# Seven-product blocks kept in three stick-breaking groups per layer, with their products in another order; attention outputs spilled unsplit; the first loads in halves

## The chip, the cores and the metric

One core of a Trainium2 chip (trn2) runs the whole program; there is one launch, and the time is device time in microseconds. The kernel before took 2468.08 us in the median of three runs (2466.44 to 2469.51). The engines are TensorE (PE, with its weight loads as PEld), VectorE (DVE), ScalarE (ACT), GpSimd (POOL) and SyncE (SP); DMAs are issued from the queues of SP, POOL and, a few, ACT.

## What is computed

Two layers on a residual stream of 256 tokens by 2048 channels, all in float32. Each layer is one normalised input, one wide input projection, two attention branches, gates, and an output projection (the reference, cut):

```python
h = rms_norm(x, norm_gain)
proj = jnp.einsum('bsd,de->bse', h, w_in)            # 10 segments of 2048 columns
(da_q, da_k, da_v, da_z, sb_q, sb_k, sb_v, sb_z, gate_a, gate_b) = split_columns(proj)
# differential attention, 8 heads: rms_norm and rope on q and k, two softmaxes per head
a = probs(qb1, k1t) - lam * probs(qb2, k2t)
ua = rms_norm(a @ v, subln_gain) * (1 - lambda_init) * jax.nn.silu(da_z)
# stick-breaking attention, 16 heads
log_fail = jnp.where(strict, jax.nn.log_sigmoid(-z), 0.0)
after = lax.cumsum(log_fail, axis=3, reverse=True) - log_fail
w = jnp.where(strict, jnp.exp(jax.nn.log_sigmoid(z) + after), 0.0)
ub = (w @ v) * jax.nn.silu(sb_z)
y = jax.nn.sigmoid(gate_a) * (ua @ w_branch_a) + jax.nn.sigmoid(gate_b) * (ub @ w_branch_b)
return x + y @ w_out
```

## The kernel before, in words

**Weights and splits.** Every projection is cut into chunks of 512 output columns: 40 of the input projection per layer, and 4 each of the two branch projections and of the output projection. A chunk is 8 tiles (`kp`) of 128 x 1024 float32, 512 KB each, which hold two contraction slices of 128. A tile is loaded into `raw` (a ring of 11), and split (L63) into a rounded high part `wh` by ACT (L64, ring of 4) and a low part `wl` by DVE (L65, ring of 3). A product is then three matmuls (`mm3`, L69 to L71) of a 128 x 128 stationary activation and 512 weight columns: high by high, high by low, low by high.

**A plain chunk** is a `c_stream` (L102): 8 tiles, each used for the two token halves, so 8 x 2 x 2 x 3 = 96 matmuls. Its two sums stand in two PSUM banks, either the pair `mc` or (with `alt`) the pair `sU`, `sN`; at its end `fin` reads them out.

**A seven-product block** is an `s_stream` (L127): two chunks are multiplied together by a recursion in two halves of the contraction, two halves of the tokens and the two chunks, with seven half products in place of eight. One product is 4 tiles x 2 slices x 3 = 24 matmuls, so a block is 168 where two plain chunks are 192. The price is sums of weights: the block loads 12 tiles from SP, and makes sums of them in place with 12 more loads from POOL that add to what lies in the tile (`add_dma`, L145 to L147), and with 4 additions on DVE (`add_w`, L208, through L151). A summed tile is split anew, so that there are 28 splits. The products, named here by bank: the first (`sU`, tile set `xs`), the second (`sN`, set `zs`), the third (`sQ`, `xs` with its first addition), the fourth (more into `sU`, `xs` with its second addition, which is issued only as the third product has split the tile), the fifth (`sQ` once more, `zs` with its addition), and the last two. The sums of the left operand lie in `sm` (`left_sums`, L303).

**The order of the work.** `run` (L222) takes one step of this and one step of that stream, in proportion to their lengths; a step is one tile. A scheduler that simulates the engines then fixes the order of the instructions on each queue, and each engine's queue runs in that order. A layer is: differential attention in four groups of heads (plain chunks one after the other, attention between them; L683 to L695); stick-breaking attention in four groups (L707 to L733), each with a seven-product block of its V and Z chunks beside two plain chunks (the next group's Q and K, in group 3 the gates a0 and a1); then the branch projections (`a_stream` L749, `b_stream` L759), with seven-product blocks of the other six gate chunks beside them (L778 to L786); then four output chunks (L825 on). So there are 7 seven-product blocks in a layer, 14 in all, and 38 plain chunks per layer.

**What goes through DRAM.** The attention outputs are split on chip and spilled as two tensors by POOL (`spill`, L495), and read back by POOL in 8 pieces per branch and layer (`reload`, L699) when buffers come free. The gates' sigmoids (`sig_d`) and the gated first branch (`ya_d`) are spilled by POOL and read back by SP (L745) in the middle of the branch stream that needs them.

**The start.** `first_input` (L333) loads the transposed input, 256 KB per step, ahead of each of the first chunk's weight tiles, and ACT and DVE scale and split it (L339, L340).

## Time and profile before

| | |
|---|---|
| runs | 2468.08 us, median of 3 (2466.44 to 2469.51) |
| the profiled execution | 2464.42 us, its span 2462.7 us, granted clock 0.988 |
| PE, PEld busy | 2384.9 us (97%), 1965.0 us (80%) |
| DVE, ACT, POOL busy | 1743.6 us (71%), 1531.9 us (62%), 393.7 us (16%) |
| DMA | 571.21 MB, mean 232 GB/s |
| matmuls and transposes on PE | 10996 |

A matmul of 512 columns is shown as some 390 ns long, but the next one starts before it ends; so the busy share of PE says little, and the distance from one start to the next is what counts. "Idle before" with a releaser names what ended a wait. The stages that the text speaks of, in us from the span's start: differential attention of layer 1 at 1231 to 1590; stick-breaking groups 0 to 2 at 440 to 735 (layer 0) and 1663 to 1955 (layer 1); from stick-breaking group 3 to the last gate block at 735 to 1080 and 1955 to 2300.

### The profile page before, as it was taken

The numbers are of one execution on the slowest core, as the hardware profiler recorded it, in microseconds if no ns is written. First come the engines' busy times: TensorE is split into PE (matmuls) and PEld (weight loads), VectorE is DVE, ScalarE is ACT, GpSimd is POOL, SyncE is SP. The second block draws the span as 40 slices with busy tenths as digits, with TensorE's granted clock in tenths as the row PEclk, the third lists the DMA queues.
The fourth block names the chain that finished last, engine by engine and source line by source line (L and its number), as shares of the span: only waits on it lengthen the run. The fifth ranks groups of instructions, "written<-read, shape, count | busy, mean of one in ns | idle before, by whom it ended". The sixth has DMA issues, their size and how long they took to land.

```text
span 2462.7 us, 31649 instructions
## 1 busy us (share of the span) xinstructions
PE 2384.9 (97%) x10996; PEld 1965.0 (80%) x10996; DVE 1743.6 (71%) x1979; ACT 1531.9 (62%) x2214; POOL 393.7 (16%) x476
## 2 busy tenths in 40 slices
PE   8999999999999999899999999999999998997999
PEld 6888888788887777688888888887888877876887
DVE  5677767688787676575666776777887876766754
ACT  6666666677777555454565676667777775655543
POOL 1132230200101211200020321302101112112000
PEclk9999999999999999899999999999999999999999
DMA  9546646888988989987665465378889889899873
GB/s 338 174 141 225 197 137 232 210 239 229 247 239 246 296 266 274 293 315 250 212 207 180 151 221 187 119 249 208 247 238 229 247 248 295 281 289 264 320 233 102
DMA packets 163040, 571.21 MB, mean 232 GB/s; under 512 B 18624, under 2 KB 19136, under 8 KB 162880
## 3 DMA queue, kind: packets, MB, share of 16 engines
q1 hardware_dynamic: 120960, 423.55, 50.8%
q0 software_dynamic: 39328, 141.58, 24.9%
q10 hardware_dynamic: 2592, 4.07, 0.5%
q8 instruction: 86, 1.41, 0.2%
q14 instruction: 74, 0.61, 0.1%
HBM read 535.57 MB, written 33.55 MB: 231 GB/s over the span
## 4 chain that ended last, share of the span: by engine, by line
PE 67%; issue 17%; DMA 7%; POOL 4%; DVE 2%; ACT 2%; POOLq 0%; SPq 0%; ACTq 0%; DVEq 0%
PE mc L69 11%; PE mc L70 11%; PE mc L71 11%; DMA raw<-in_w_in 6%; PE sU L70 4%; PE sN L70 4%; PE sU L71 4%; PE sN L71 4%; PE sN L69 4%; PE sU L69 4%; POOL raw L147 2%; PE at L243 2%; PE sQ L70 1%; PE sQ L69 1%; PE sQ L71 1%
## 5 line engine op out<-in xcount | busy, mean ns | idle before, releaser
L65 DVE TENSOR_TENSOR wl<-raw,wh 128x1024 fp32r<-128x1024 f32 x1000 | 1209.8, 1222 | 495.3 <-PE mc L70 158.9
L64 ACT CAST wh<-raw 128x1024 fp32r<-128x1024 f32 x1000 | 1045.9, 1053 | 724.4 <-PE mc L71 280.9
L147 POOL DMA_DIRECT2D raw<-in_w_in x168 | 145.5, 868 | 743.0 <-DVE wl L65 466.3
L70 PE MATMUL mc<-wl,xTh 128*128 128x512 f32 x576 | 225.9, 392 | 0.4 <-DVE wl L65 0.2
L71 PE MATMUL mc<-wh,xTl 128*128 128x512 f32 x576 | 225.0, 391 | 0.0
L69 PE MATMUL mc<-wh,xTh 128*128 128x512 f32 x576 | 207.0, 394 | 5.5 <-ACT tok L465 3.4
L69 PE MATMUL mc<-wh,xrh 128*128 128x512 f32 x512 | 198.6, 392 | 8.6 <-ACT wh L64 8.5
L70 PE MATMUL mc<-wl,xrh 128*128 128x512 f32 x512 | 201.8, 394 | 1.8 <-DVE wl L65 1.8
L71 PE MATMUL mc<-wh,xrl 128*128 128x512 f32 x512 | 200.9, 392 | 0.0
L69 PEld LDWEIGHTS mc<-wh,xTh 128*128 128x128 f32 x576 | 107.8, 189 | 29.9 <-ACT wh L64 4.3
L70 PEld LDWEIGHTS mc<-wl,xTh 128*128 128x128 f32 x576 | 108.5, 188 | 25.6 <-DVE wl L65 3.5
L71 PEld LDWEIGHTS mc<-wh,xTl 128*128 128x128 f32 x576 | 108.5, 188 | 21.7
L69 PEld LDWEIGHTS mc<-wh,xrh 128*128 128x128 f32 x512 | 96.4, 189 | 29.3 <-ACT wh L64 9.5
L70 PEld LDWEIGHTS mc<-wl,xrh 128*128 128x128 f32 x512 | 96.6, 189 | 23.3 <-DVE wl L65 3.7
L71 PEld LDWEIGHTS mc<-wh,xrl 128*128 128x128 f32 x512 | 96.6, 189 | 19.2
L252 POOL TENSOR_SCALAR rv<-ssq 128x4 f32<-128x4 f32 (+1 forms) x48 | 40.2, 837 | 419.4 <-ACT junk L433 379.4
L70 PE MATMUL sU<-wl,xrh 128*128 128x512 f32 x256 | 100.6, 393 | 1.1 <-DVE wl L65 1.1
L71 PE MATMUL sN<-wh,xrl 128*128 128x512 f32 x256 | 100.5, 393 | 0.0
L70 PE MATMUL mc<-wl,ua 128*128 128x512 f32 x256 | 100.2, 391 | 0.2 <-DVE wl L65 0.2
L71 PE MATMUL sU<-wh,xrl 128*128 128x512 f32 x256 | 100.2, 391 | 0.0
L69 PE MATMUL sN<-wh,xrh 128*128 128x512 f32 x256 | 100.1, 391 | 0.0
L70 PE MATMUL sN<-wl,xrh 128*128 128x512 f32 x256 | 99.9, 390 | 0.0
(258 smaller groups left out, 5010.6 us busy)
## 6 DMA issues: line engine op xcount, KB each, us to landing
raw<-in_w_in SPq DMA_DIRECT2D x584, 512.0 KB, 4.4
raw<-in_w_in POOLq DMA_DIRECT2D x168, 512.0 KB, 9.7
raw<-in_w_a SPq DMA_DIRECT2D x64, 512.0 KB, 5.7
raw<-in_w_b SPq DMA_DIRECT2D x64, 512.0 KB, 5.8
raw<-in_w_o SPq DMA_DIRECT2D x64, 512.0 KB, 4.3
uah<-uh POOLq DMA_DIRECT2D x8, 512.0 KB, 4.9
ual<-ul POOLq DMA_DIRECT2D x8, 512.0 KB, 6.9
ubh<-uh POOLq DMA_DIRECT2D x8, 512.0 KB, 6.4
```

What stands on the lines that cost most here:

```text
L64: nc.scalar.copy(h, src)
L65: nc.vector.tensor_tensor(out=l, in0=src, in1=h.bitcast(F32), op=ALU.subtract)
L69: nc.tensor.matmul(ps, lhsT=lh, rhs=rh, start=start, stop=False, **kw)
L70: nc.tensor.matmul(ps, lhsT=lh, rhs=rl, start=False, stop=False, **kw)
L71: nc.tensor.matmul(ps, lhsT=ll, rhs=rh, start=False, stop=stop, **kw)
L147: nc.gpsimd.dma_start(out=dst, in_=src, accum_op=ALU.add)
L243: nc.tensor.transpose(out=tr[:, j * P:(j + 1) * P], in_=src[:, j * P:(j + 1) * P], identity=ident)
L252: nc.gpsimd.tensor_scalar(out=v[:, :w], in0=ss, scalar1=1.0 / n, scalar2=RMS_EPS, op0=ALU.mult, op1=ALU.add)
```

## The change

1. Seven-product blocks stay only in stick-breaking groups 0 to 2: 3 in a layer, 6 in all. Group 3's Z and V and all eight gate chunks become plain chunks, one stream at a time: Z, V, then gate a0, branch a0, gate a1, branch a1 and so on, then the same for b. A layer has 46 plain chunks.
2. In a seven-product block the product with `zs` that came fifth comes fourth, ahead of the one that adds to `sU`; it uses bank `sQ` again, right after the third product, whose result ACT copies out (L215).
3. Attention outputs are spilled as one float32 tensor, half the bytes. They are read back by SP into the `raw` ring and split then (one ACT and one DVE instruction per 512 KB). The last stick-breaking group's output isn't spilled; it stays on chip as the split pair, and branch b's streams start their contraction with it.
4. The first weight tile is loaded and split in two halves, the first input tile too, and DVE in place of ACT makes the high part of the latter.
5. The `raw` ring has 12 buffers, `ev` shares the `pp` ring of 5, and a doubled set of constants is gone.

```diff
-RAW = 11
+RAW = 12
...
+    def held(nm):
+        return wp.tile([P, CW], F32, name="pp", bufs=PPB)
...
+    def first_slice(src, between):
+        raw = raw_tile()
+        h = wp.tile([P, KK * CW], F32R, name="wh", bufs=4)
+        l = wp.tile([P, KK * CW], F32R, name="wl")
+        for i in range(KK):
+            c = slice(i * CW, (i + 1) * CW)
+            nc.sync.dma_start(out=raw[:, c], in_=src[:, c])
+            if i == 0:
+                between()
+            with tc.high_priority(offset=400):
+                split(h[:, c], l[:, c], raw[:, c])
+        return h, l
...
-    def c_stream(src, lhs, fin, alt=False, gap=0, before=None):
+    def c_stream(src, lhs, fin, alt=False, gap=0, before=None, first=False, depth=range(KP)):
...
-        for kp in range(KP):
-            if before is not None:
-                before(kp)
-            h, l = split_raw(load_raw(src[kp]))
+        for i, kp in enumerate(depth):
+            if first and i == 0:
+                h, l = first_slice(src[kp], lambda: before(0))
+            else:
+                if before is not None:
+                    before(i)
+                h, l = split_raw(load_raw(src[kp]))
...
-    def s_stream(sl, sr, xh, sm, fin):
+    def s_stream(sl, sr, xh, sm, fin, tb_dma=False):
...
         q_ps = ps_s.tile([P, CW], F32, name="sQ")
-        yield from prod(q_ps, s(0), lambda i: xs[i], lambda i: add_dma(xs[i], b22[i]))
+        yield from prod(q_ps, s(0), lambda i: xs[i], next_sums)
         p5 = held("p5")
         nc.scalar.copy(p5, q_ps)
         yield
+        if tb_dma:
+            v_ps = ps_s.tile([P, CW], F32, name="sQ")
+            yield from prod(v_ps, s(2), lambda i: zs[i], None, False)
+            yield
 
         yield from prod(u_ps, s(1), lambda i: xs[i], None, True)
...
-        v_ps = ps_s.tile([P, CW], F32, name="sQ")
-        yield from prod(v_ps, s(2), lambda i: zs[i], None, False)
+        if not tb_dma:
+            v_ps = ps_s.tile([P, CW], F32, name="sQ")
+            yield from prod(v_ps, s(2), lambda i: zs[i], None, False)
...
         def spill(b, g, u):
-            for i in range(2):
-                nc.gpsimd.dma_start(out=u_dram[b][i][:, g * 4:(g + 1) * 4], in_=u[i])
+            nc.gpsimd.dma_start(out=u_dram[b][:, g * 4:(g + 1) * 4], in_=u)
...
         def reload(b, groups, u):
             for g in groups:
+                raw = load_raw(u_dram[b][:, g * 4:(g + 1) * 4].rearrange("p h s -> p (h s)"))
+                ts = [att.tile([P, 4, S], F32R, name="u" + b, tag=tag) for tag in GZ_TAGS[g]]
+                split(ts[0], ts[1], raw.rearrange("p (h s) -> p h s", s=S))
                 for i in range(2):
-                    ut = att.tile([P, 4, S], F32R, name="u" + b, tag=GZ_TAGS[g][i])
-                    nc.gpsimd.dma_start(out=ut, in_=u_dram[b][i][:, g * 4:(g + 1) * 4])
-                    u[i].append(ut)
+                    u[i][g] = ts[i]
...
             if g + 1 < NG:
-                c = chain(q_stream(NG + g + 1, xt, False, GAP), k_stream(NG + g + 1, xt, False, GAP))
+                s = s_stream(w_chunk(SB_V, g), w_chunk(SB_Z, g), xt, sm,
+                             lambda col, t, op: (fv, fz)[col](t, op), True)
+                c = chain(q_stream(NG + g + 1, xt, False, GAP),
+                          k_stream(NG + g + 1, xt, False, GAP))
+                run((2 * (C_STEPS + GAP), c), (S_STEPS, s))
             else:
-                c = chain(c_stream(w_chunk(GATE_A, 0), xt, sig_fin("a", 0), False, GAP),
-                          c_stream(w_chunk(GATE_A, 1), xt, sig_fin("a", 1), False, GAP))
-            run((2 * (C_STEPS + GAP), c), (S_STEPS, s))
...
+                run((1, c_stream(w_chunk(SB_Z, g), xt, out_of(fz))))
+                run((1, c_stream(w_chunk(SB_V, g), xt, out_of(fv), True)))
+            last_u = sb_out(g, wT, v, gzT[0])
...
-            return c_stream([w_b[l, c, kp] for kp in range(KP)], ub, fin, alt, gap, before)
+            return c_stream([w_b[l, c, kp] for kp in range(KP)], ub, fin, alt, gap, before,
+                            depth=[KP - 2, KP - 1, *range(KP - 2)])
...
-        run((2 * (C_STEPS + GAP), chain(a_stream(0, False, GAP), a_stream(1, False, GAP))),
-            (S_STEPS, gate_block("a", 2)))
-        run((2 * (C_STEPS + GAP), chain(a_stream(2, False, GAP), a_stream(3, False, GAP))),
-            (S_STEPS, gate_block("b", 0)))
-        reload("b", range(NG), ub)
-        late = gate_block("b", 2)
...
+        for c in range(NG):
+            run((1, gate_chunk("a", c, c % 2 == 0)))
+            run((1, a_stream(c, c % 2 == 1)))
+        for c in range(NG):
+            run((1, gate_chunk("b", c, c % 2 == 0)))
+            if c == 0:
+                reload("b", range(NG - 1), ub)
+            run((1, b_stream(c, c % 2 == 1)))
```

**How the queues move.** On PE, in a seven-product block: the end of the third product and what follows it, in layer 0's stick-breaking group 0. `sQ_4431` and `sU_4213` are the third and the fourth product's banks before; now the third is `sQ_4410`, and `sQ_4513` is the product with `zs`. `at` are small attention matmuls. Before:

```order
L70 MATMUL sQ_4431<-wl_4522,smh_3662 128x512
L71 MATMUL sQ_4431<-wh_4521,sml_3663 128x512
L69 MATMUL sU_4213<-wh_4534,smh_3662 128x512
L70 MATMUL sU_4213<-wl_4535,smh_3662 128x512
L71 MATMUL sU_4213<-wh_4534,sml_3663 128x512
L69 MATMUL sU_4213<-wh_4534,smh_3662 128x512
```

And in the changed kernel:

```order
L70 MATMUL sQ_4410<-wl_4501,smh_3645 128x512
L71 MATMUL sQ_4410<-wh_4500,sml_3646 128x512
L536 MATMUL at_4156<-ident_313,tok_4144 128x128 x4
L69 MATMUL at_4163<-kTh_4023,qTh_3857 128x256
L70 MATMUL at_4163<-kTl_4024,qTh_3857 128x256
L71 MATMUL at_4163<-kTh_4023,qTl_3858 128x256
L69 MATMUL at_4163<-kTh_4023,qTh_3857 128x256
L70 MATMUL at_4163<-kTl_4024,qTh_3857 128x256
L71 MATMUL at_4163<-kTh_4023,qTl_3858 128x256
L69 MATMUL sQ_4513<-wh_4514,smh_3645 128x512
```

Ten small matmuls, then the product with `zs`, now stand behind the third product, where the product into `sU` came at once; that one starts 46 rows later than the third's last row (it came one row later before).

On SP, in the branch a stage of layer 0 (`in_w_a` is the branch's weight, `in_w_in` the gates', `siga_*` the spilled sigmoids of one gate chunk). Before, around the first two branch chunks:

```order
L88 DMA raw<-in_w_a 128x1024
L745 DMA tok<-siga_371 128x512 x2
L88 DMA raw<-in_w_a 128x1024 x7
L88 DMA raw<-in_w_in 128x1024 x2
L88 DMA raw<-in_w_a 128x1024
L88 DMA raw<-in_w_in 128x1024
L88 DMA raw<-in_w_a 128x1024
```

And in the changed kernel, from gate a0's 8 tiles on:

```order
L91 DMA raw<-in_w_in 128x1024 x8
L91 DMA raw<-in_w_a 128x1024 x8
L91 DMA raw<-in_w_in 128x1024 x7
L789 DMA tok<-siga_366 128x512
L91 DMA raw<-in_w_in 128x1024
L789 DMA tok<-siga_366 128x512
L91 DMA raw<-in_w_a 128x1024 x8
L91 DMA raw<-in_w_in 128x1024 x7
L789 DMA tok<-siga_367 128x512
```

The gates' tiles and the branch's tiles are no longer mixed, and the read of a gate's sigmoids stands behind all 8 tiles of the branch stream that needs it and 7 tiles of the next gate.

More of the change, by code (lines that the diff above doesn't have):

```diff
@@ L118, in c_stream @@
                 mm3(ps[t], at_k(lhs[0], k)[:, ts], at_k(lhs[1], k)[:, ts], h[:, cs], l[:, cs],
-                    k == 0, k == KT - 1)
-            if kp < KP - 1:
+                    i + kk == 0, i == KP - 1 and kk == KK - 1)
+            if i < KP - 1:
                 yield
@@ L171, in loader @@
             return get
-        def held(nm):
-            return wp.tile([P, CW], F32, name="pp", bufs=PPB)
         u_ps = ps_s.tile([P, CW], F32, name="sU")
@@ L183, in s_stream, with next_sums @@
         n_ps = ps_s.tile([P, CW], F32, name="sN")
-        yield from prod(n_ps, s(3), loader(zs, b22), lambda i: add_dma(zs[i], b12[i]))
+        yield from prod(n_ps, s(3), loader(zs, b22),
+                        (lambda i: add_dma(zs[i], b12[i])) if tb_dma else None)
         yield
+        def next_sums(i):
+            if tb_dma:
+                add_dma(xs[i], b22[i])
+            else:
+                add(xs[i], zs[i])
+                add_dma(zs[i], b12[i])
         q_ps = ps_s.tile([P, CW], F32, name="sQ")
-        yield from prod(q_ps, s(0), lambda i: xs[i], lambda i: add_dma(xs[i], b22[i]))
+        yield from prod(q_ps, s(0), lambda i: xs[i], next_sums)
         p5 = held("p5")
@@ L322, in left_sums @@
         return sm
-    ident = const.tile([P, P], F32, name="ident")
-    make_identity(nc, ident)
-    mhalf = const.tile([P, 4], F32, name="mhalf")
-    nc.gpsimd.memset(mhalf, -0.5)
     xr = slot("C", "xr")
@@ L334, in first_input @@
         raw = tok()
-        nc.sync.dma_start(out=raw, in_=xT[:, kp * CW:(kp + 1) * CW])
+        if kp:
+            nc.sync.dma_start(out=raw, in_=xT[:, kp * CW:(kp + 1) * CW])
         for j in range(KK):
@@ L338, in first_input @@
             rv = raw[:, j * S:(j + 1) * S]
-            nc.scalar.mul(xr[0][:, k], rv, gcol[:, k:k + 1])
+            if kp:
+                nc.scalar.mul(xr[0][:, k], rv, gcol[:, k:k + 1])
+            else:
+                nc.sync.dma_start(out=rv, in_=xT[:, k * S:(k + 1) * S])
+                nc.vector.tensor_scalar(out=xr[0][:, k], in0=rv, scalar1=gcol[:, k:k + 1],
+                                        scalar2=None, op0=ALU.mult)
             nc.vector.scalar_tensor_tensor(out=xr[1][:, k], in0=rv, scalar=gcol[:, k:k + 1],
@@ L353, in trunk @@
     run((1, c_stream([w_in[0, DA_Q, kp] for kp in range(KP)], xr, lambda ps: first.update(ps=ps),
-                     before=first_input)))
+                     before=first_input, first=True)))
     sums_of_squares()
@@ L411, in w_chunk @@
             return [w_in[l, base + g, kp] for kp in range(KP)]
-        u_dram = {b: [dram.tile([P, KT, S], F32R, name=f"u{b}{p}") for p in "hl"] for b in "ab"}
+        u_dram = {b: dram.tile([P, KT, S], F32, name=f"u{b}") for b in "ab"}
         qT, kT = {}, {}
@@ L424, in fin @@
                 for t in range(NT):
-                    ns.append(work.tile([P, CW], F32, name="ev", bufs=2))
+                    ns.append(held("ev"))
                     with tc.high_priority(offset=100):
@@ L489, in attn_pair, with u_parts @@
                     att.tile([P, HPG, 3, P], F32R, name="aTl"))
-        def u_stage():
+        def u_parts():
             return (att.tile([P, HPG, S], F32R, name="uh", tag="aTh"),
@@ L596, in da_out @@
                                                    op1=ALU.mult)
-            us = u_stage()
+            us = att.tile([P, HPG, S], F32, name="us", tag="aTh")
             for t in range(NT):
@@ L600, in da_out @@
                 nc.vector.tensor_tensor(out=u, in0=hold[:, t], in1=gz[:, t], op=ALU.mult)
-                put_T(u, us, 0, t)
+                tr = ps_at.tile([P, CW], F32, name="at")
+                for j in range(HPG):
+                    nc.tensor.transpose(out=tr[:, j * P:(j + 1) * P], in_=u[:, j * P:(j + 1) * P],
+                                        identity=ident)
+                nc.scalar.copy(us[:, :, t * P:(t + 1) * P], heads(tr))
             spill("a", g, us)
@@ L626, in sb_out @@
         def sb_out(g, wT, v, gzT):
-            us = u_stage()
+            keep = g == NG - 1
+            if keep:
+                uh, ul = u_parts()
+            else:
+                us = att.tile([P, HPG, S], F32, name="us", tag="aTh")
             for hp in range(0, HPG, 2):
@@ L638, in sb_out @@
                         False, True)
-                u = tok()
-                uv = u.rearrange("p (h q) -> p h q", q=S)
-                nc.vector.tensor_tensor(out=uv, in0=ov, in1=gzT[:, hp:hp + 2], op=ALU.mult)
-                split(us[0][:, hp:hp + 2], us[1][:, hp:hp + 2], uv)
+                hs = slice(hp, hp + 2)
+                uv = tok().rearrange("p (h q) -> p h q", q=S) if keep else us[:, hs]
+                nc.vector.tensor_tensor(out=uv, in0=ov, in1=gzT[:, hs], op=ALU.mult)
+                if keep:
+                    split(uh[:, hs], ul[:, hs], uv)
+            if keep:
+                return uh, ul
             spill("b", g, us)
@@ L648, in trunk @@
         ya_d = [dram.tile([P, NT, CW], F32, name=f"ya{c}") for c in range(NG)]
-        def put_sig(b, c, t, g):
-            nc.scalar.activation(out=g, in_=g, func=AF.Sigmoid)
-            nc.gpsimd.dma_start(out=sig_d[b, c][:, t], in_=g)
         def sig_fin(b, c):
@@ L659, in fin @@
                     nc.gpsimd.dma_start(out=sig_d[b, c][:, t], in_=g)
-            return fin
-        def sig_s_fin(b, c0):
-            def fin(col, t, op):
-                g = tok()
-                op(g)
-                put_sig(b, c0 + col, t, g)
             return fin
```

29 lines of the change are left out of this document (14 added, 15 removed).

## The prediction

> **What bounds the kernel now.** I began with the profile's page, for what the engines do overall and what one instruction of each kind costs.
>
> ```profile
> span 2462.7 us, 31649 instructions
> PE 2384.9 (97%) x10996; PEld 1965.0 (80%) x10996; DVE 1743.6 (71%) x1979; ACT 1531.9 (62%) x2214; POOL 393.7 (16%) x476
> ...
> L65 DVE TENSOR_TENSOR wl<-raw,wh 128x1024 fp32r<-128x1024 f32 x1000 | 1209.8, 1222 | 495.3 <-PE mc L70 158.9
> L64 ACT CAST wh<-raw 128x1024 fp32r<-128x1024 f32 x1000 | 1045.9, 1053 | 724.4 <-PE mc L71 280.9
> ```
>
> TensorE is the bound: DVE and ACT, the next busiest, wait for it most. How much of its time is work is not in the 97%, since matmuls overlap. So I took the distance between starts from the timeline of the second layer's output projection, where nothing waits (first and last of 19 rows):
>
> ```profile
> 2399.77 0.39 PE L69 MATMUL sU<-wh,yTh 128*128 128x512 f32 x1
> ...
> 2403.85 0.39 PE L69 MATMUL sU<-wh,yTh 128*128 128x512 f32 x1
> ```
>
> 18 steps in 4.08 us: a weight matmul costs 0.2267 us. Then the busy time by stage (length, then each engine's busy us and number of instructions, PE's clock, DMA share, GB/s), and the same for the instructions that touch `wh` alone. Of each three weight matmuls two read `wh`, so their number is 1.5 times the second table's PE count.
>
> ```profile
> 440.00:735.00 295.00, 291.17 (x1417) 241.70 (x1416) 236.02 (x257) 210.30 (x266) 39.95 (x50) 1.00 0.87 233
> 735.00:1080.00 345.00, 319.15 (x1367) 258.29 (x1367) 242.81 (x233) 205.70 (x222) 61.69 (x87) 0.95 0.94 279
> 1231.00:1590.00 359.00, 359.00 (x1696) 299.37 (x1695) 245.89 (x317) 236.02 (x464) 84.99 (x81) 1.00 0.56 183
> 1663.00:1955.00 292.00, 288.68 (x1408) 240.12 (x1407) 232.88 (x251) 208.15 (x262) 38.43 (x48) 1.00 0.86 234
> 1955.00:2300.00 345.00, 316.10 (x1370) 254.49 (x1370) 244.18 (x235) 207.37 (x225) 61.73 (x87) 0.97 0.94 277
> ```
>
> ```profile
> 440.00:735.00 295.00, 234.44 (x746) 139.64 (x746) 164.19 (x137) 141.25 (x136) 1.00 0.87 233
> 735.00:1080.00 345.00, 278.74 (x870) 168.59 (x869) 195.13 (x164) 170.69 (x164) 0.95 0.94 279
> 1231.00:1590.00 359.00, 302.35 (x975) 182.10 (x974) 147.54 (x122) 127.38 (x122) 1.00 0.56 183
> 1663.00:1955.00 292.00, 232.22 (x740) 138.50 (x740) 162.93 (x135) 141.22 (x135) 1.00 0.86 234
> 1955.00:2300.00 345.00, 276.44 (x874) 166.06 (x873) 194.62 (x162) 169.46 (x163) 0.97 0.94 277
> ```
>
> The differential stage of layer 1 (1231 to 1590) has plain chunks only and PE busy throughout. It is my standard: 1462 weight matmuls x 0.2267 = 331.4 us, and the other 27.6 us for 234 small ones, 0.118 us each. By these two prices the others lose:
>
> - 735 to 1080: 1305 x 0.2267 + 62 x 0.118 = 303.1 of 345, so 41.9 us lost.
> - 1955 to 2300: 1311 x 0.2267 + 59 x 0.118 = 304.2 of 345, so 40.8 lost.
> - 440 to 735: 1119 x 0.2267 + 298 x 0.118 = 288.9 of 295, so 6.1 lost.
> - 1663 to 1955: 1110 x 0.2267 + 298 x 0.118 = 286.8 of 292, so 5.2 lost.
>
> What is lost shows in the timeline of one gap (PE), and in the page of line 147, the loads that add:
>
> ```profile
> 1027.58 0.39 PE L71 MATMUL mc<-wh,ub 128*128 128x512 f32 x1
> 1037.31 0.79 PE L69 MATMUL sU<-wh,smh 128*128 128x512 f32 x1 [9.34 <-ACT wh L64]
> ...
> 1040.02 0.63 PE L70 MATMUL sU<-wl,smh 128*128 128x512 f32 x1
> 1040.45 0.63 PE L71 MATMUL sU<-wh,sml 128*128 128x512 f32 x1
> ```
>
> ```profile
> 1036.21 1.05 ACT L64 CAST wh<-raw 128x1024 fp32r<-128x1024 f32 x1 [13.08 <-DMA raw<-in_w_in]
> 1037.17 0.58 ACT L190 COPY pp<-sQ 128x512 f32<-128x512 f32 x1
> ```
>
> ```profile
> DMA to landing us min/median/max: 5.1/9.7/20.9
> ```
>
> The fourth product needs its second addition, ACT sits 13.08 us before that split, the additions take up to 20.9 us, and PE stands for 9.34 us; behind the gap its matmuls start 0.43 us apart for a while, not 0.227. The 14 blocks are not alike: the 8 in the two late stages lose 82.7 / 8 = 10.3 us each, the 6 in the early ones 11.3 / 6 = 1.9 us each. A block saves 24 matmuls, 5.4 us. So the late ones cost more than they save, and the early ones pay.
>
> **The change part by part.** *Eight blocks become plain chunks.* It adds 8 x 24 = 192 matmuls: + 43.5 us, all on the path, since PE is the bound. It removes 8 x 12 = 96 additions by DMA from POOL, 8 x 12 = 96 splits and 32 DVE additions, and with them the waits in the two late stages: - 82.7 us. What the plain chunks lose in place of that is in my standard already (a stage of plain chunks with attention between them); the bounds of this term are new waits, next.
>
> *Hand-overs between streams.* In the new order a stream often takes the bank pair that the stream before it has just filled (V to gate a0, branch a0 to gate a1, and so on): 8 times in a layer, 16 in all. The read-out is then between the two. Two rows bound it, the hand-over from branch b3 to the output projection, both in `mc`, and the longest PE wait for such a read-out in group 0 of the stick-breaking stage:
>
> ```profile
> 1147.13 0.39 PE L71 MATMUL mc<-wh,ub 128*128 128x512 f32 x1
> 1147.36 0.39 PE L69 MATMUL mc<-wh,yTh 128*128 128x512 f32 x1
> ```
>
> ```profile
> PE mc L69 <- ACT tok L465: 1.7, 1, 1.7
> ```
>
> From 0 to 1.7 us each, so 0 to 27 us. The last tile of a stream finishes its first bank six matmuls (1.4 us) ahead of the second, as it does at the hand-over without a gap, and this one is the same form; I take 0.3 each, + 5 us.
>
> *The other order in the kept blocks.* The second addition now has the whole `zs` product before it is needed: 46 rows on PE's queue, over 10 us at 0.2267, beside the 9.7 us of the median. The product with `zs` loses some of its own head start but keeps the third product in front. Its new wait, for ACT's copy out of `sQ` (0.58 us above), has ten attention matmuls in front of it, 1.2 us. The gain is bounded by the 11.3 us that these stages lose, of which 1.7 per layer is the read-out wait above, which the order doesn't touch; the other bound is nothing, or the same again lost if the `zs` tiles are late instead. I take - 7 us.
>
> *Spills and reloads.* Seven read-backs per layer now need a split each, 14 x 1.05 us on ACT and 14 x 1.22 on DVE. In a plain stage DVE is busy 245.88 of 359 and ACT 236.02, so they are covered; without cover they would be worth at most some 17 us. Half the spilled bytes, and the splits of all outputs but the last group's, go from engines that are off the path too. Branch b used to begin with four read-backs through POOL; it now begins with the pair that never left. That wait is in the 82.7 already. Behind SP's read of the sigmoids stand the next tiles; SP is twelve tiles, 12 x 12 x 0.2267 = 33 us of PE work, ahead, so I cost its wait at nothing.
>
> *The first loads in halves.*
>
> ```profile
> 6.36 1.05 ACT L64 CAST wh<-raw 128x1024 fp32r<-128x1024 f32 x1 [0.59 <-DMA raw<-in_w_in]
> ...
> 27.18 1.05 ACT L64 CAST wh<-raw 128x1024 fp32r<-128x1024 f32 x1 [3.11 <-DMA raw<-in_w_in]
> ```
>
> The first split can start one or two us sooner, but ACT still waits 3.11 us for a weight tile at 27 us: loads set the pace there, and their bytes are the same. I take 0, between -2 and 0.
>
> **The sum** on the profiled span: 2462.7 + 43.5 - 82.7 + 5 - 7 = 2421.5 us. The profiled execution (2464.42) lies 1.7 us above its span, and the runs' median (2468.08) 3.7 above the profiled execution. So 2423.2 for an execution, and **2427 us** for the median.
>
> How much of the loss is real is the crux, and here a page speaks. The Trainium skill's "Perfetto Trace Analysis", section "Identifying the Most-Contended Engine", calls the busy share of matmuls a bad measure and points to the share of weight loads. By PE's busy time the two late stages lose only 25.9 + 28.9 = 54.8 us, and the sum would come to 2455; by weight loads, with the standard's 299.37 of 359 as full, they need 258.29 and 254.49 over 0.834, or 309.7 and 305.1, and lose 75.2, which makes 2434. The trace sides with the page: the slow matmuls after a gap count as busy.
>
> **The rivals.** *The kept blocks gain nothing* (the `zs` tiles are late in place of the `xs` ones): 2427 + 7 = 2434. For it: ACT's queue is in order, so any late split holds the plain stream's too. Against it: 46 rows of head start.
>
> *The hand-overs cost the full 1.7 us*: 2427 + 22 = 2449. For it: the one row of 1.7 us. Against it: the b3 hand-over.
>
> *The sigmoids' round trip comes too late, and the kernel is slower.* The place is the read-out of each of the 16 branch streams, which multiplies by sigmoids that the gate stream just before it made; before, they had been made a stage earlier.
>
> ```profile
> siga<-tok POOLq DMA_DIRECT2D x16, 256.0 KB, 5.2
> tok<-siga SPq DMA_DIRECT2D x16, 256.0 KB, 7.6
> ```
>
> Spill and read take 5.2 + 7.6 = 12.8 us by these medians, and a branch stream lasts 96 x 0.2267 = 21.8 us, so 9 are to spare. If the read comes late in SP's queue or both take twice as long (25.6), PE waits 3.8 us and then restarts slowly, some 2 us more as in the gap above: 16 x 5.8 = 93 us, or 2520. It decides from 41 / 16 = 2.6 us per branch stream on. The place of the read, seven tiles into the next gate, speaks for it; SP's lead of 33 us speaks against.
>
> *The extra matmuls get a lower clock*, so that the saved waits buy nothing: at a granted clock of 0.97 over the two late stages (some 780 us) 24 us more, 2451. The standard's 359 us without a pause at 1.00 speak against it. *Or the change doesn't do what it says* and the waits come from the DMA traffic as such, not from the additions: then plain chunks beside reloads at 0.94 of DMA's share would keep, say, half of the 82.7, and the time is 2468, no change. But a block loads 24 tiles where two plain chunks load 16, so the traffic goes too.
>
> **How the numbers follow.** Forecast 0.66, kept blocks gain nothing 0.12, costly hand-overs 0.10, lower clock 0.03, half of the waits stay 0.04, round trip 0.05. Measurement tells no change from 0.2%, 4.9 us, apart: 2463.1 to 2473.0. Faster is the first four, 0.91; the fifth is the same, 0.04; slower 0.05. The range reaches down to the kept blocks' full 11.3, free hand-overs and the start's 2 us (2427 - 4 - 5 - 2 = 2416, and some us for the edges of the windows), up to the costly hand-overs: 2410 to 2450.
>
> **What would show it.** Right: matmuls on PE are up by 192; from the last kept block to the output projection PE is busy without a pause, at 0.2267 us a weight matmul and a granted clock of 1.00, and each layer's 18 plain chunks there take about 392 us and their attention; line 147's successor issues 72 additions; waits of PE for `wh` in `sU` products are gone; the stick-breaking stages lose 2 us per layer, not 5 or 6. Wrong: gaps on PE at the start of gate streams (hand-overs) or at the end of branch streams (round trip), a wait of the `zs` product for `wh`, or a late stage whose loads, not PE, set the pace.

## The result and the profile after

The changed kernel takes **2422.08 us** (median of 4 runs, 2420.9 to 2424.16); the kernel before took 2467.26 us in the same comparison (4 runs, 2464.07 to 2469.51). The ratio is 0.9819, with a 95% interval of 0.9802 to 0.9836: 45 us less. The forecast was 2427 us, in 2410 to 2450. The profiled execution took 2422.19 us and its span is 2420.4 us, where the prediction's sum was 2421.5; the granted clock over the span is 0.999, where it was 0.988.

The head of the page of the changed kernel, and its row of the loads that add, which are now 72:

```profile
span 2420.4 us, 31313 instructions
PE 2399.4 (99%) x11188; PEld 1993.4 (82%) x11188; DVE 1583.4 (65%) x1800; ACT 1429.7 (59%) x2099; POOL 279.7 (12%) x327
...
L167 POOL DMA_DIRECT2D raw<-in_w_in x72 | 61.9, 859 | 474.7 <-DVE wl L65 316.0
```

PE has 11188 - 10996 = 192 more instructions, the eight blocks' 24 each. The busy time by stage of the changed kernel follows (columns as in the prediction's tables): first the two late stages, which now end at 1127 and 2328 us, then the two early ones; and behind it the late stages once more, for the instructions that touch `wh` (in the early stages these matmuls number 755 and 760).

```profile
735.00:1127.00 392.00, 390.79 (x1763) 324.25 (x1762) 207.19 (x193) 185.34 (x198) 16.94 (x30) 1.00 0.72 235
1935.00:2328.00 393.00, 390.92 (x1763) 324.30 (x1763) 206.99 (x192) 185.15 (x198) 15.87 (x28) 1.00 0.70 232
440.00:735.00 295.00, 292.61 (x1431) 244.59 (x1430) 234.01 (x253) 211.53 (x264) 34.92 (x43) 1.00 0.84 230
1640.00:1935.00 295.00, 293.79 (x1438) 246.13 (x1437) 235.22 (x253) 212.85 (x265) 34.53 (x43) 1.00 0.84 230
```

```profile
735.00:1127.00 392.00, 346.69 (x1122) 210.23 (x1121) 171.06 (x141) 147.37 (x140) 1.00 0.72 235
1935.00:2328.00 393.00, 346.68 (x1122) 210.44 (x1122) 171.05 (x140) 147.25 (x140) 1.00 0.70 232
```

By the prediction's two prices a late stage is 1683 weight matmuls x 0.2267 and 80 small ones x 0.118, or 390.9 us: 1.1 us lost of 392 and 2.1 of 393, 3.2 in all, where it was 82.7. The early stages lose 295 - 291.9 = 3.1 and 295 - 293.6 = 1.4, 4.5 in all, where it was 11.3. So the span's 42.3 us come out as + 43.5 (more matmuls) - 79.5 (late stages) - 6.8 (early stages) = - 42.8, and half a microsecond besides. The start alone lost more than that: the weight matmul behind the first 600 starts at 159.12 us, where it was 156.78 before, with 54 small matmuls ahead of it in both kernels. The other 1.8 us, by difference, were won in the rest of the program.

All waits of PE in the changed kernel of 1 us and more (what PE waited for: us in total, times, longest), and below them the longest sum of the kernel before:

```profile
PE mc L69 <- DVE xrh L371: 5.0, 1, 5.0
PE mc L70 <- DVE wl L65: 4.5, 7, 1.0
PE mc L69 <- ACT wh L64: 2.9, 3, 2.2
PE sU L69 <- DVE tok L799: 2.1, 1, 2.1
PE sU L69 <- ACT wh L64: 1.2, 1, 1.2
PE sQ L69 <- ACT pp L216: 1.0, 2, 0.5
```

```profile
PE sU L69 <- ACT wh L64: 44.0, 11, 9.7
```

The first is the program's start. The fourth is a hand-over between streams, the last the new wait for the copy out of `sQ`. Of the 44 us of `sU` products waiting for `wh`, 1.2 are left.

### The profile page after: what moved, and what is told of

Same layout as the page of the kernel before. It is cut to its first block, busy times and chain, and to the rows that moved or that the text cites. A ratio compares the mean times of both kernels' runs of the same rounds, so it can differ in the third digit from the quotient of the medians.

```text
span 2420.4 us, 31313 instructions
## 1 busy us (share of the span) xinstructions
PE 2399.4 (99%) x11188; PEld 1993.4 (82%) x11188; DVE 1583.4 (65%) x1800; ACT 1429.7 (59%) x2099; POOL 279.7 (12%) x327
## 5 line engine op out<-in xcount | busy, mean ns | idle before, releaser
L65 DVE TENSOR_TENSOR wl<-raw,wh 128x1024 fp32r<-128x1024 f32 (+1 forms) x905 | 1101.1, 1223 | 640.4 <-PE mc L70 253.0
L64 ACT CAST wh<-raw 128x1024 fp32r<-128x1024 f32 (+1 forms) x905 | 947.9, 1051 | 802.4 <-PE mc L71 403.1
L70 PE MATMUL mc<-wl,xTh 128*128 128x512 f32 x768 | 299.8, 390 | 2.4 <-DVE wl L65 2.4
L71 PE MATMUL mc<-wh,xTl 128*128 128x512 f32 x768 | 299.2, 390 | 0.0
L69 PE MATMUL mc<-wh,xTh 128*128 128x512 f32 x768 | 283.5, 391 | 0.2 <-ACT wh L64 0.2
L70 PEld LDWEIGHTS mc<-wl,xTh 128*128 128x128 f32 x768 | 144.2, 188 | 33.0 <-DVE wl L65 3.7
L69 PEld LDWEIGHTS mc<-wh,xTh 128*128 128x128 f32 x768 | 143.6, 188 | 29.9 <-ACT wh L64 0.9
L167 POOL DMA_DIRECT2D raw<-in_w_in x72 | 61.9, 859 | 474.7 <-DVE wl L65 316.0
L69 PE MATMUL sU<-wh,xrh 128*128 128x512 f32 x256 | 100.0, 391 | 0.0
L69 PE MATMUL sU<-wh,xTh 128*128 128x512 f32 x240 | 94.3, 393 | 3.3 <-DVE tok L799 2.1
```

The costliest lines, as they stand in the source:

```text
L64: nc.scalar.copy(h, src)
L65: nc.vector.tensor_tensor(out=l, in0=src, in1=h.bitcast(F32), op=ALU.subtract)
L69: nc.tensor.matmul(ps, lhsT=lh, rhs=rh, start=start, stop=False, **kw)
L70: nc.tensor.matmul(ps, lhsT=lh, rhs=rl, start=False, stop=False, **kw)
L71: nc.tensor.matmul(ps, lhsT=ll, rhs=rh, start=False, stop=stop, **kw)
L167: nc.gpsimd.dma_start(out=dst, in_=src, accum_op=ALU.add)
```

## The experiments

Three theories of what the late blocks lost were tested. A, the prediction's reading: the second addition is needed too soon after it is issued, which is a matter of the order. B: the additions fill the DMA engines, so that all loads and sums come late. C: the blocks hold too many `raw` buffers. Beside them stand the terms of the sum. Each kernel was compared with runs of the kernel before on the same chip (median there 2464 to 2466 us), and its ratio is to those.

**The order alone, in all 14 blocks of the kernel before.**

```diff
+        v_ps = ps_s.tile([P, CW], F32, name="sQ")
+        yield from prod(v_ps, s(2), lambda i: zs[i], None, False)
+        yield
         yield from prod(u_ps, s(1), lambda i: xs[i], None, True)
...
-        yield
-        v_ps = ps_s.tile([P, CW], F32, name="sQ")
-        yield from prod(v_ps, s(2), lambda i: zs[i], None, False)
```

> The kernel before with one edit: in all 14 seven-product blocks the product with the zs tiles comes fourth, ahead of the one that adds to sU. Blocks, spills and start as before. Theory A (the late blocks lose because the second addition is needed too soon): the waits of PE for wh in sU products go, and most of the 82.7 us lost in the two late stages with them, at least half: the time is 2420 or less, and the 14 blocks keep their saved matmuls. Theory B (the late blocks lose because their loads are too many beside the plain chunks, DMA share 0.94 there): the late stages still lose 60 us or more, and the time is 2445 to 2462.

Measured: 2467.6 us, ratio 1.0007 (0.9998 to 1.0017). The late stages of this kernel, then its early ones, and PE's waits in the first late stage:

```profile
735.00:1080.00 345.00, 318.45 (x1376) 256.59 (x1376) 246.30 (x237) 209.77 (x226) 62.19 (x87) 0.97 0.94 280
1955.00:2300.00 345.00, 318.86 (x1402) 258.04 (x1401) 246.06 (x237) 208.42 (x226) 63.42 (x89) 0.98 0.94 280
440.00:735.00 295.00, 288.30 (x1398) 239.16 (x1397) 232.56 (x251) 206.79 (x260) 38.90 (x48) 0.99 0.84 230
1663.00:1955.00 292.00, 285.57 (x1369) 237.71 (x1368) 230.31 (x247) 206.33 (x259) 37.60 (x47) 0.99 0.83 228
```

```profile
PE mc L69 <- ACT wh L64: 12.0, 5, 7.5
PE mc L70 <- DVE wl L65: 10.7, 8, 2.9
PE sU L69 <- ACT wh L64: 1.1, 2, 0.6
```

With 876 and 875 matmuls on `wh` the two late stages still lose 39.8 + 36.9 = 76.7 us. The waits of `sU` are gone, as the new order promises, and waits of nearly the same sum stand in `mc`, the plain chunks beside the blocks. Theory A falls: the product that waits only shows the lateness, it doesn't make it. The unchanged time hides a loss, too: the early stages (733 and 736 on `wh`) lose 10.6 + 10.5 = 21.1 us, where it was 11.3, so in this kernel the new order costs there more than it gains in the late stages.

**More buffers alone** (the kernel before with the change's ring of 12, and `ev` in the `pp` ring).

```diff
-RAW = 11
+RAW = 12
...
-                    ns.append(work.tile([P, CW], F32, name="ev", bufs=2))
+                    ns.append(held("ev"))
```

> The kernel before with 12 raw buffers (and ev in the pp ring, which makes the room). In the changed kernel one buffer is worth 9 us. Theory C (the late blocks lose because they hold raw tiles for long and leave the plain chunks too few): one buffer more takes 15 us or more off the late stages, 2450 or less. Theory B (their loads keep the DMA engines full): the late stages stay within 8 us, 2455 to 2466.

Measured: 2466.47 us, ratio 1.0003 (0.9992 to 1.0015). By their counts (874 and 872 on `wh`) the late stages lose 40.2 + 41.1 us, and PE's wait of the `sU` products for `wh` is this row:

```profile
PE sU L69 <- ACT wh L64: 45.3, 10, 9.7
```

Theory C falls for the late blocks.

**The same loads without the addition.** In the four late blocks of each layer of the kernel before, every load that adds becomes a plain load of the same bytes into the same tile, from the same queue and behind the same waits. The sums of weights in these blocks are left out.

```diff
         def add_dma(dst, src):
             with tc.high_priority(offset=400):
-                nc.gpsimd.dma_start(out=dst, in_=src, accum_op=ALU.add)
+                if late:
+                    nc.gpsimd.dma_start(out=dst, in_=src)
+                else:
+                    nc.gpsimd.dma_start(out=dst, in_=src, accum_op=ALU.add)
```

> The kernel before, with the additions by DMA of its eight late blocks made plain loads of the same bytes into the same tiles, after the same waits; the sums are left out there. By the profile POOL's queue takes 24.9% of the DMA engines for 141.58 MB and SP's 50.8% for 423.55, so 1.5 times as much for a byte. If it is the adding that fills the engines, the share falls to 0.87 or less and a third or more of the 83 us goes, 2440 or less. If it is the bytes, or what waits for them: 2455 to 2468.

Measured: 2401.82 us, ratio 0.9743 (0.9727 to 0.9758). Its late stages (961 and 963 matmuls on `wh`):

```profile
735.00:1080.00 345.00, 339.66 (x1514) 278.14 (x1513) 263.88 (x254) 221.04 (x240) 47.06 (x88) 1.00 0.86 308
1955.00:2300.00 345.00, 339.51 (x1504) 278.22 (x1503) 257.82 (x245) 211.80 (x224) 44.62 (x83) 0.99 0.85 303
```

335.3 + 334.5 us of matmuls by the two prices: 9.7 + 10.5 = 20.2 us are lost, where it was 82.7. (This kernel is some 30 us ahead in layer 1, so the second window starts inside the stage; the span, 60.8 us shorter, says the same: 21.9 are left.) The DMA engines now move 308 and 303 GB/s at 0.86 and 0.85 of their time, where the kernel before moved 279 and 277 at 0.94. So the traffic in bytes was not the limit; the addition was. The blocks themselves then lose 20.2 / 8 = 2.5 us each, near the early blocks' 1.9, and save 5.4.

**Half of each addition.** In the same blocks the loads add to the first half of each tile only; the other half of the added sums is left out.

```diff
         def add_dma(dst, src):
+            if late:
+                dst, src = dst[:, :CW], src[:, :CW]
```

> The kernel before, with the additions by DMA of its eight late blocks on the first half of each tile only, 256 KB in place of 512; order, waits and buffers as before, and half of the added sums is left out. Theory B: the load on the DMA engines in the late stages falls from 0.94 to some 0.85, and at least half of the 83 us lost there goes, 2425 or less. Theory C or A: the products wait for the same things, 50 us or more stay lost, 2440 or more.

Measured: 2402.5 us, ratio 0.9746 (0.973 to 0.9761), with 960 and 960 matmuls on `wh` in the late stages:

```profile
735.00:1080.00 345.00, 339.73 (x1511) 277.71 (x1511) 263.77 (x254) 220.63 (x239) 62.55 (x88) 1.00 0.88 274
1955.00:2300.00 345.00, 340.04 (x1504) 277.94 (x1503) 257.78 (x246) 211.65 (x226) 56.50 (x82) 0.99 0.86 275
```

10.2 + 11.0 = 21.2 us lost: halving the additions does as much as making all of them plain. POOL's own work is not the reason: it is busy for 62.55 us in the first late stage, where it was 61.69. But POOL's loads also land sooner than before. Their rows in the first late stage (size, median us from issue to landing) are shown for the kernel before and the one with plain loads; the 45 half additions take 7.1 us:

```profile
raw<-in_w_in POOLq DMA_DIRECT2D x45, 512.0 KB, 12.0
```

```profile
raw<-in_w_in POOLq DMA_DIRECT2D x45, 512.0 KB, 7.4
```

So these two runs show that the additions cause the loss. Whether full engines make it, or the late sums by themselves, they don't tell; the next experiment is for that. The row of the queue from which POOL's loads go (packets, MB, share of 16 DMA engines over the span) gives their price; it is shown for the kernel before, for this one, and for the one with plain loads:

```profile
q1 hardware_dynamic: 120960, 423.55, 50.8%
q0 software_dynamic: 39328, 141.58, 24.9%
```

```profile
q0 software_dynamic: 39328, 116.41, 20.9%
```

```profile
q0 software_dynamic: 39328, 141.58, 20.7%
```

The kernel before spends 0.249 x 2462.7 = 613 us of all 16 engines on q0. With plain loads it is 0.207 x 2401.9 = 497, so an addition costs 116 / 96 = 1.2 us more than a plain load. With half additions it is 0.209 x 2402.7 = 502, so half an addition is 111 / 96 = 1.16 us, and a whole one some 2.3. A plain load of 512 KB on q1 takes 0.508 x 2462.7 / 808 = 1.55 us (423.55 MB are as much as 808 loads), and 1.55 + 1.2 is 2.8. An adding load thus takes 2.3 to 2.8 us of all engines, one and a half to nearly two plain ones. This is an estimate, since the time of a packet may hold some waiting when the engines are crowded. By the same count the engines are busy for 0.94 x 345 = 324 us in a late stage of the kernel before, whose matmuls need 303 or 304, so in these stages the engines come nearer to being the bound than PE does. The Trainium skill's "DMA: Bandwidth & Descriptors", section "Rules for kernel authors", says that an accumulating DMA reads its destination and writes it later. The surplus agrees with a transfer that touches its tile twice, but no run here separates the read from the write.

**Additions that nobody waits for.** The loads that add in the six gate blocks (72 of the late 96) go into three spare tiles, whose turn is tied to the block by a copy of one column on POOL; the sums of these blocks are left out. The `raw` ring keeps 11 buffers, and `ev` shares the `pp` ring to make room. A first form has the copies on DVE.

```diff
         def add_dma(dst, src):
+            if aside:
+                aside.append(aside.pop(0))
+                nc.gpsimd.tensor_copy(aside[0][:, :1], dst[:, :1])
+                dst = aside[0]
             with tc.high_priority(offset=400):
```

> The kernel before, with the additions by DMA of its six gate blocks sent to three spare tiles, so that no product waits for them; the same bytes go through the same queue, and the sums are left out of the gates. Theory B (amount of loads): the late stages still lose 60 us or more of the 83, 2445 to 2468. Rival (the wait for the additions' landing, which the other order only moved to the plain streams through ACT's and DVE's queues): the six blocks' part goes, 2400 to 2415.

> The kernel before, with the additions of its six gate blocks sent to three spare tiles as in the run with additions aside, but tied to their place by a one-column copy on POOL, so that DVE's queue never waits for them; sums left out of the gates. Theory B (the engines' load): 60 us or more of the 83 stay lost, 2445 to 2468. Theory A (the products wait for the additions): those blocks' part goes, 2400 to 2420.

Measured: with the copies on DVE 2466.82 us, ratio 1.0005 (0.9994 to 1.0017); on POOL 2447.37 us, ratio 0.9928 (0.9905 to 0.9951). The first is confounded; DVE, whose queue is in order, stood at the tying copies. Between 735 and 1130 us of that kernel:

```profile
DVE dummy L154 <- DMA dummy<-in_w_in: 23.2, 15, 4.1
DVE dummy L154 <- DMA raw<-in_w_in: 19.9, 11, 3.9
```

The form with the copies on POOL, its late stages (901 and 896 matmuls on `wh`) and a wait of its own:

```profile
735.00:1080.00 345.00, 328.80 (x1415) 266.79 (x1414) 251.80 (x241) 212.46 (x231) 82.84 (x130) 0.96 0.96 288
1955.00:2300.00 345.00, 323.83 (x1408) 263.63 (x1408) 247.92 (x235) 207.15 (x223) 82.34 (x127) 0.96 0.96 290
```

```profile
PE mc L69 <- DMA ua<-uah: 10.0, 2, 7.3
```

31.1 + 32.8 = 63.9 us are still lost, though no product of these six blocks needs an added sum. Up to 10 us of that come from reloads that now stand behind the copies in POOL's queue. The plain loads from SP are later than they were: in the first late stage those of `in_w_in`, `in_w_a` and `in_w_b` land in 7.0, 6.6 and 8.0 us (medians), where it was 5.5, 5.7 and 5.9 in the kernel before and 5.2, 5.1 and 5.4 with plain loads from POOL. So most of the loss stays when the additions load the engines (share 0.96) and nobody waits for them, and some goes with the dependence on them. Theory B holds in the main. How the rest divides between the lateness of the sums and that of plain tiles isn't settled: the copies disturb the queue by about as much as is left to divide. A version that makes the late blocks' sums in another way, from plain loads, was not tried.

**Plain traffic in the changed kernel** (ring of 11; an idle 512 KB load on POOL beside every second tile of gate and branch streams, with a one-column copy on DVE to tie it).

```diff
+                if extra and i % 2 == 0:
+                    d = wp.tile([P, KK * CW], F32, name="dummy", bufs=1)
+                    nc.vector.tensor_copy(d[:, :1], raw[:, :1])
+                    nc.gpsimd.dma_start(out=d, in_=src[kp])
```

> The changed kernel with one idle load of 512 KB through POOL, into a tile that nobody reads, for every second weight tile of the gate and branch streams: 4 per stream, 64 per layer, so that a pair of gate and branch streams (43.5 us of matmuls) moves 24 tiles and not 16; the raw ring is 11. Nothing waits for these loads. Theory B (the late blocks lost to the amount of loads, at a DMA share of 0.94 and 280 GB/s): the late stages, now at 235 GB/s and 0.72, reach that share and lose 20 us or more each: 2460 or more. Rival (what is lost needs someone who waits for the additions): within 5 us of the kernel with 11 buffers.

Measured: 2477.15 us, ratio 1.0045 (1.0024 to 1.0065). Two views of this kernel: the busy time in the first late stage and the longest sum of waits on DVE there:

```profile
735.00:1127.00 392.00, 371.71 (x1633) 303.91 (x1632) 195.29 (x236) 171.56 (x182) 45.65 (x85) 0.98 0.83 295
```

```profile
DVE dummy L136 <- issue: 63.6, 20, 5.5
```

This run doesn't decide between the theories: the tying copies hold DVE's queue, and PE waits mostly for read-outs behind them (36.0 us by L805 and L815 over the span), less for `wl` (11.6). It shows only that 295 GB/s of plain loads leave the engines at 0.83.

**The order, in the changed kernel** (its six blocks in the old order; the inverse of the first experiment).

```diff
-        if tb_dma:
-            v_ps = ps_s.tile([P, CW], F32, name="sQ")
-            yield from prod(v_ps, s(2), lambda i: zs[i], None, False)
-            yield
         yield from prod(u_ps, s(1), lambda i: xs[i], None, True)
...
+        v_ps = ps_s.tile([P, CW], F32, name="sQ")
+        yield from prod(v_ps, s(2), lambda i: zs[i], None, False)
```

> The changed kernel with the old order of the products in its six blocks. By the prediction's term the other order is worth 7 us, by the trace of after some 9: 2429 to 2431, with the waits in sU products of groups 0 to 2 back. Rival (the six blocks gained from the change of what is around them, such as half the spills, not from the order): 2422 to 2424.

Measured: 2427.06 us, ratio 0.9844 (0.9824 to 0.9864); the span is 2425.2 us, 4.8 longer than the changed kernel's. The intervals of the two ratios overlap, but the trace has the difference where it should be: by their counts (749 and 752 matmuls on `wh`) the early stages lose 5.1 + 4.2 us, where the changed kernel loses 4.5. The waits of `sU` products that were expected back aren't seen; PE waits 0.2 us for `wh` there. In the kernel before, the same order gained nothing.

**One `raw` buffer, in the changed kernel.**

```diff
-RAW = 12
+RAW = 11
```

> The changed kernel with the raw ring at 11 in place of 12. The other order of the products gained nothing in the kernel before and 5 us in the changed one, which has one buffer more. If the buffer makes that difference, the early stages lose some 5 us more: 2426 to 2428. If not (half the spills, or what stands around the blocks): 2422.

Measured: 2431.27 us, ratio 0.9867 (0.9852 to 0.9882), span 2429.7: the twelfth buffer is worth 9 us here, and in the kernel before it was worth nothing. That is more than was expected, since the late stages lose too. These are the stages of this kernel (1117, 1112, 751 and 755 matmuls on `wh`):

```profile
735.00:1127.00 392.00, 388.92 (x1755) 322.67 (x1754) 204.90 (x190) 184.54 (x198) 17.00 (x30) 1.00 0.71 233
1935.00:2328.00 393.00, 389.68 (x1754) 323.20 (x1753) 207.18 (x196) 185.79 (x200) 15.06 (x27) 1.00 0.70 228
440.00:735.00 295.00, 291.18 (x1424) 243.27 (x1423) 233.87 (x253) 210.88 (x263) 35.00 (x43) 1.00 0.83 230
1640.00:1935.00 295.00, 292.00 (x1426) 244.13 (x1425) 231.53 (x246) 210.47 (x262) 34.92 (x43) 1.00 0.83 228
```

The late stages lose 2.8 + 4.7 us where 12 buffers lose 3.2, the early ones 4.5 + 3.6 where 12 buffers lose 4.5. With the same ring of 11 and the same order the kernel before lost 21.1 in its early stages, so the buffer isn't all that makes the order pay here; the rest (half the spilled bytes, `ev` in another ring, other neighbours) was not tried alone.

**The hand-overs** (strict turns: gates always in one pair of banks, branches in the other) **and the first loads** (whole again), each alone in the changed kernel.

```diff
-            run((1, gate_chunk("a", c, c % 2 == 0)))
-            run((1, a_stream(c, c % 2 == 1)))
+            run((1, gate_chunk("a", c, False)))
+            run((1, a_stream(c, True)))
```

> The changed kernel with the bank pairs of the gate and branch streams in strict turns (gates in mc, branches in sU and sN), so that no stream of these takes the pair that the stream before it has just filled. By the trace of after the hand-overs cost some 4 us in all (one of about 2 us per layer, from branch a1 to gate a2): 2418 to 2419, and no PE wait for the read-out of a branch. If that wait has another cause than the shared bank: 2422.

```diff
-    run((1, c_stream([w_in[0, DA_Q, kp] for kp in range(KP)], xr, lambda ps: first.update(ps=ps),
-                     before=first_input, first=True)))
+    run((1, c_stream([w_in[0, DA_Q, kp] for kp in range(KP)], xr, lambda ps: first.update(ps=ps),
+                     before=first_input)))
...
-        if kp:
-            nc.sync.dma_start(out=raw, in_=xT[:, kp * CW:(kp + 1) * CW])
+        nc.sync.dma_start(out=raw, in_=xT[:, kp * CW:(kp + 1) * CW])
```

> The changed kernel with the first loads whole, as before. The traces say that halves let the first matmul start 2.5 us sooner (4.99 for 7.46) but that matmul number 96 comes 2 us later (38.10 for 36.08). If the halves cause the later loss, the time falls by 1 to 2 us (2420 to 2421) and matmul 96 comes near 36 us. If the loss comes from something else in the start (the order of ACT's queue, one buffer more), matmul 96 stays near 38 us, and the time is 2422 to 2424.

Measured: strict turns 2419.53 us (2417.96 to 2420.1), ratio 0.9813 (0.9798 to 0.9829), and the wait of `sU` for the read-out at L799 is gone; whole first loads 2420.49 us (2417.14 to 2422.9), ratio 0.9817 (0.98 to 0.9835). Both medians lie some 2 us below the changed kernel's, but the intervals of the ratios overlap with its own. The stages and the start tell more than the time does. With strict turns PE has no gap in the late stages:

```profile
735.00:1127.00 392.00, 392.00 (x1770) 325.60 (x1769) 207.67 (x194) 185.94 (x200) 17.01 (x30) 1.00 0.70 235
1935.00:2328.00 393.00, 393.00 (x1774) 326.41 (x1774) 209.46 (x195) 186.29 (x199) 15.93 (x28) 1.00 0.69 235
```

With 1126 and 1129 matmuls on `wh` their work is 392.4 and 393.4 us by the two prices, so the 3.2 us that the changed kernel loses there are gone, and a little more. The span gains only 2.6, as the start of this run is 0.6 us later (159.68 against 159.12 for the weight matmul behind the first 600) and its first early stage loses 0.8 more. Of the first loads: halves begin PE's work 2.5 us sooner (4.99 us from the span's start, 7.46 before), but the second chunk starts 2 us later: 38.10 us, where it was 36.08 before and is 36.28 with whole loads. This is not made up later: the weight matmul behind the first 600 starts at 159.12 us with halves and at 158.12 with whole loads. But these are single traces, and strict turns, which leave the first loads alone, move the same point by 0.6 us. Halves are not all of it either: with them and 11 `raw` buffers the second chunk starts at 36.66.

**ACT's queue at the start** (strict turns, and the eight loads of `x` for the sums of squares go out from POOL, not from ACT).

```diff
-                nc.scalar.dma_start(out=xc, in_=x[t * P:(t + 1) * P, c * CW:(c + 1) * CW])
+                nc.gpsimd.dma_start(out=xc, in_=x[t * P:(t + 1) * P, c * CW:(c + 1) * CW])
```

> The changed kernel with bank pairs in strict turns and the eight loads of x for the sums of squares issued by POOL, not by ACT, whose splits stood behind them in the first 40 us. If ACT's queue made the loss there, matmul 96 comes at 33 us in place of 38 and the time is 2414 to 2416. If the loads as such set the pace of the first 40 us, it comes at 37 to 38 and the time is that of strict turns alone, 2418 to 2420.

Measured: **2412.44 us** (2412.12 to 2412.55), ratio 0.9793 (0.9777 to 0.981), the lowest time here of a kernel that leaves nothing out. The interval of its ratio still overlaps a little with the changed kernel's, so the trace has to say where the time went. In the changed kernel ACT issues these loads between its splits; from its timeline (start, duration, and in brackets the idle time before with what ended it):

```profile
15.47 1.05 ACT L64 CAST wh<-raw 128x1024 fp32r<-128x1024 f32 x1
...
19.45 0.33 ACTq L382 DMA_DIRECT2D tok<-in_x  x1
19.83 1.05 ACT L64 CAST wh<-raw 128x1024 fp32r<-128x1024 f32 x1 [2.49 <-DMA tok<-in_x]
...
25.56 0.33 ACTq L382 DMA_DIRECT2D tok<-in_x  x1
25.93 1.04 ACT L64 CAST wh<-raw 128x1024 fp32r<-128x1024 f32 x1 [4.25 <-DMA raw<-in_w_in]
```

A load goes out only when its buffer is free, and each split stands behind it: none starts from 15.47 to 19.83 and again to 25.93. With the loads on POOL splits start at 15.88, 18.53, 21.15 and 23.80, and the second chunk's first matmul, in the two kernels, moves 7.75 us:

```profile
38.10 0.39 PE L69 MATMUL sU<-wh,xrh 128*128 128x512 f32 x1
```

```profile
30.35 0.39 PE L69 MATMUL sU<-wh,xrh 128*128 128x512 f32 x1
```

From strict turns alone this kernel differs only in these loads: the weight matmul behind the first 600 starts at 152.28 us, where it is 159.68 there, and the span is 2417.8 - 2410.6 = 7.2 us shorter. The amount of bytes isn't what held the splits: in the first 24 us the queue of SP's loads moved 7.39 MB in the changed kernel and 6.82 MB in this one, which had then started all eight splits of the first chunk.

## Why the prediction was right, and where its account was not

**The bound and the prices.** Right: 192 matmuls more on PE, the late stages at 0.2267 us a weight matmul and a clock of 1.00, 392 and 393 us where about 392 was said.

**Eight blocks become plain chunks, + 43.5 - 82.7.** The size was right (79.5 of the 82.7, since plain chunks lose 3.2 of their own), the reason only in part. "The fourth product needs its second addition" described one gap; with the order changed in the kernel before the loss stayed at 76.7 us and moved to other products. What cost the time is the additions by DMA, shown by making them plain or half as large: 20.2 and 21.2 us lost. In the main it is what they take of the DMA engines, since 63.9 us stay lost where nobody waits for three in four of them; that run isn't clean, so this second step is shown less well than the first. The forecast came through because removing a block removes its additions under either account. The rival that blamed "the DMA traffic as such" was nearer in its cause, but bytes are not it: 308 GB/s without additions lost a quarter of what 279 with them did. Why the early blocks lost so little was not told by the prediction at all. Its own tables had it: 0.87 and 0.86 of the engines' time there, 0.94 in the late stages; that this headroom is the reason is argued, and no run moved it. The weighing by the Trainium skill's "Perfetto Trace Analysis", section "Identifying the Most-Contended Engine", stands: by busy time 54.8 us could be won there, by weight loads 75.2, and 79.5 were.

**Hand-overs, + 5.** About right: the late stages lose 3.2 us, and with strict turns none, so the hand-overs cost 3 to 4 us, 2.1 of them in one wait. The full 1.7 us at each of 16 didn't happen.

**The other order, - 7.** The early stages lose 6.8 us less (3.1 and 1.4 us are left, where 2 per layer was said), but not by the order alone, and that the sum came so near is luck in part. In the changed kernel the order is worth 4.8; in the kernel before, the bound that the prediction also named, the same again lost, came true: 21.1 us in place of 11.3. What the sum left out is the surroundings, the ring of 12 among them. With 11 buffers the new kernel's early stages lose 8.1 us in place of 4.5 and its late ones 7.5 in place of 3.2. The standard stage, which the prediction took as free of loss for plain chunks, would not have held in the late stages with the old ring.

**Spills and reloads, 0.** No wait of 1 us and more names them. This part was not tried alone, and it may have a share in what the order is worth. The sigmoids' round trip did not show either: no branch stream waits for its sigmoids, and the rival falls for this kernel.

**First loads in halves, 0 (between - 2 and 0).** Not a gain: by one trace of each, halves cost 1.0 us (159.12 against 158.12), outside these bounds, though the same point also moves by 0.6 where the first loads stay as they are. The whole start, with its other changes, lost 2.3. The second chunk was late by more than the first was early. The step held that the loads' bytes set the pace; ACT's queue did: its row of 3.11 us before the split at 27 us stands right behind a load that ACT issued itself, and in the changed kernel moving those loads off ACT brought the second chunk 7.75 us forward.

**From the sum to the median.** The span was forecast at 2421.5 and came out at 2420.4. Most of the 5 us between 2427 and 2422 is the 3.7 that the profiled execution before lay under its median; the one after lies at its median.

## What to carry to other kernels

Before you lay a stage's loss to the instruction that waits, look at what share of time the DMA engines are busy there beside the GB/s: 0.94 at 279 GB/s said that transfers of an expensive kind, not bytes, filled them. A saving on the bound engine that is paid for with adding loads should be placed where the engines have room, and a wait taken away in a full stage comes back on the next tile. When engines wait in order, look at who issues a load, too: a load that waits for its buffer holds back every later instruction of its engine.

## What the runs showed that was not expected

- A load of 512 KB that adds takes an estimated 2.3 to 2.8 us of all 16 DMA engines, a plain one 1.55; 96 of the former made plain were worth 63 us of 2465.
- The same buffer is worth nothing in one kernel (2466.47 with it, 2465.03 without) and 9 us in another (2422 with it, 2431 without), and the same order of products costs 9.8 us in the early stages of one kernel and saves 4.8 in those of the other.
- Eight small loads on ACT's queue cost some 7 us at the start of the program.
